# SSD output projection of a hybrid decoder layer: seven products of quarters in place of eight, with the sums of activations made by GpSimd group by group

## The chip, the cores and the metric

One core of a Trainium2 chip runs the whole program in one launch. The metric is the device time of one execution in microseconds (us). A core has a tensor engine (TensorE, PE in the rows; PEld is its weight loading), a vector engine (VectorE, DVE), a scalar engine (ScalarE, ACT), GpSimd (POOL) and SyncE (SP). Here SP only issues DMA transfers; POOL and ACT issue some too. Each engine works through its own instructions in order and waits on semaphores for the others.

## The reference

The reference is one decoder layer on x of 1024 tokens by 1024 channels: a Mamba-2 SSD branch and a latent-attention branch, merged by gates, then a gated MLP. The part that is edited:

```python
y_ssd = ssd_mixer(...) @ w_ssd_proj[i]       # (1024 tokens, 2048) @ (2048, 1024)
y_mla = mla_mixer(...) @ w_mla_proj[i]
g_ssd, g_mla = jnp.split(jax.nn.sigmoid(gates + gate_b[i]), 2, axis=-1)
x = x + (g_ssd * y_ssd + g_mla * y_mla) @ w_o[i]
```

`ssd_mixer` ends in an RMS norm over each of four groups of 512 channels: a group's 512 rows of the projection's input are final once its scan over the tokens is done.

## The kernel before

Activations lie with channels on the partitions and tokens along the row. A matrix product in f32 is made of three matmuls in f32r (`mm3`, L174): each operand is split into a rounded part `hi` and a rest `lo` (ACT casts, DVE or GpSimd subtracts, `split`, L152), and hi·hi, hi·lo and lo·hi are added in PSUM. The rows of TensorE therefore come in threes, L175 to L177, each 128x128 weights against 128x512 activations.

The stages around the change, in the order of time in the profile:

- **SSD scan** (to about 1262 us). Four groups of channels, each in eight chunks of 128 tokens (`ssd_steps`). TensorE is filled in between by "background" work: the convolution inputs of the next group, the z tiles, the attention's output projection (`mla_tiles`). The order within this stage is fixed by how many background steps `advance` takes per step of the scan; the instructions of each engine stand in the order in which the code emits them. When half a group's tokens are scanned, `ssd_finish(g, half)` sums squares, takes the inverse root (DVE, L119 to L125), transposes it (L955) and scales the group's four 128x512 tiles (L957). Half 0 of the last group is split at once and stays on chip; all other halves are stored to `y_d` in DRAM by SP (L965), four stores of 256 KB.
- **SSD output projection** (about 1253 to 1475). Eight output tiles of 128 channels for each half of the tokens. One tile is 16 steps over the 2048 input channels, 48 matmuls. Half 0 has its activations (`ya0`) loaded and split during the attention projection; its first tile runs as background while the last group is normalised (`first_ssd_tile`). Half 1's are loaded from `y_d` and split between the halves (`load_act`). Weights: `load_w` brings 256 KB pieces through two `wraw` buffers (L160) and splits them.
- **Gates and merge.** Each tile's result is multiplied by its gate (`gt`, loaded from `g_d` by GpSimd, L1214), the attention's part is added (`mt` from `m_d`, L1216) and the sum is split (`ma`, `m`).
- **w_o** for that half of the tokens: eight steps over channels for each half of the outputs, added to x (L1270), squares summed, the result `x2` stored to `x_d` (L1280). So the order is: projection half 0, w_o half 0, projection half 1, w_o half 1. The second norm's scaling of half 0 (`norm`, L255) is emitted ahead of w_o half 1, and reads and overwrites the tile that the store to `x_d` reads.
- **MLP up and down**, which already uses seven products of quarters (`Pair`, `w_sums`, `w_split`); its first raw weights are loaded by `w_raw` into the pool `up`.

The pool `up`, opened after the SSD stage, lies over memory that the stage's pool `dp` frees; what is loaded into it waits for whatever still uses that memory. Hardware DMA transfers of SP take turns on eight semaphore lanes: a transfer waits for the one eight before it, so at most eight are outstanding.

Of the kernel before, what the change touches and what calls it, by code (L numbers as in the profile page):

```python
# [9 lines left out]
F32 = mybir.dt.float32  # L10
# [62 lines left out]
def tile_hybrid_layer(ctx: ExitStack, tc: tile.TileContext, x, cols, cons, w_main, w_small, w_uq, w_ukv,  # L73
# [14 lines left out]
    l_d = dram.tile([4 * MH, 256], F32, name="l_d")  # L88
    y_d = dram.tile([2 * D, T], F32, name="y_d")
    z_d = dram.tile([2 * D, T], F32, name="z_d")  # L90
# [82 lines left out]
    def mm3(ps, a, b, first, last, **more):  # L173
        (ah, al), (bh, bl) = a, b  # L174
        PE.matmul(ps, lhsT=ah, rhs=bh, start=first, stop=False, **more)  # L175
        PE.matmul(ps, lhsT=ah, rhs=bl, start=False, stop=False, **more)  # L176
        PE.matmul(ps, lhsT=al, rhs=bh, start=False, stop=last, **more)  # L177

    def act_tile():
# [592 lines left out]
    with tc.tile_pool(name="dp", bufs=2) as dp, tc.tile_pool(name="psx", bufs=1, space=PSUM) as psx, \  # L772
# [166 lines left out]
        def ssd_finish(g, half):  # L939
# [16 lines left out]
            for j in range(4):  # L956
                V.scalar_tensor_tensor(x[:, j, s], x[:, j, s], col(CG_SSDG + 4 * g + j), np_,  # L957
                                       op0=ALU.mult, op1=ALU.mult)
# [35 lines left out]
        def mla_tiles():  # L994
# [11 lines left out]
            def y_step(j):  # L1006
# [5 lines left out]
                if j < 24 and j % 2 == 0:  # L1012
                    k = j // 2
                    raw = dp.tile([P, 512], F32, name="nb") if 4 <= k < 6 else \
                        dp.tile([P, 8, P], F32, name="abc", bufs=3).rearrange("p a b -> p (a b)")[:, 0:512] if k > 8 else \
                        lt.tile([P, 512], F32, name="lt")
                    staged.append(raw_load(y_d, k, hs_(0), raw))

# [32 lines left out]

        def first_ssd_tile():
            ws = [load_w(w_ssd[0, kp], [P, KD, P]) for kp in range(2)]
            ps = lin_tile()
            head.append(ps)
            for k in range(16):
                while ya0[k] is None:
                    yield False
                hi, lo = ws[k // KD]
                mm3(ps, (hi[:, k % KD, :], lo[:, k % KD, :]), (ya0[k][:, 0, :], ya0[k][:, 1, :]), k == 0, k == 15)  # L1060
                yield True

# [38 lines left out]
        w_eng[0] = V  # L1101
        background.append(first_ssd_tile())
        while fins:
# [65 lines left out]
    with tc.tile_pool(name="ep", bufs=2) as ep:  # L1169
        x2b = []  # L1170
        with tc.tile_pool(name="em", bufs=2) as em:
# [31 lines left out]

            m0 = [em.tile([P, 2, 512], F32R, name="ma", bufs=3) for _ in range(3)]
            for half in range(2):
                if half:
                    w_raw(q0, loaded)
                    w_raw(q1, loaded)
                s = hs_(half)
                ya = ya0 if half == 0 else [load_act(y_d, k * P, s) for k in range(16)]  # L1210
                ms = []
                for ct in range(8):
                    gt = em.tile([P, 512], F32, name="gt")
                    nc.gpsimd.dma_start(out=gt, in_=g_d[ct * P:(ct + 1) * P, s])  # L1214
                    mt = em.tile([P, 512], F32, name="mt")
                    nc.gpsimd.dma_start(out=mt, in_=m_d[ct * P:(ct + 1) * P, s])  # L1216
                    if half == 0 and ct == 0:
                        ps = head[0]
                    else:
                        ps = lin_tile()  # L1220
                        drain([steps([load_w(w_ssd[ct, kp], [P, KD, P]) for kp in range(2)], ya, ps, range(16), 16)])
                    if ct == 5:
                        loaded = last(mybir.EngineType.SP)
                    V.scalar_tensor_tensor(gt, gt, 1.0, ps, op0=ALU.add, op1=ALU.mult)
                    V.tensor_tensor(gt, gt, mt, op=ALU.add)  # L1225
                    m = em.tile([P, 2, 512], F32R, name="m", bufs=5) if ct >= 3 else \
                        em.tile([P, 2, 512], F32R, name="ma", bufs=3) if half else m0[ct]
                    S.mul(m[:, 0, :], gt, 0.5)
                    V.scalar_tensor_tensor(m[:, 1, :], gt, 0.5, m[:, 0, :].bitcast(F32), op0=ALU.mult, op1=ALU.subtract)
                    ms.append(m)  # L1230
                if half:
                    x0 = [x2b[0][:, i, :] for i in range(4)]
                    drain([norm(x0, x0, ep, x2ss[0])])
                big = ep.tile([P, 4, D], F32, name="x2")
                x2b.append(big)
                nc.sync.dma_start(out=big, in_=x[s, :].rearrange("(i p) c -> p i c", p=P))
                behind(loaded)
                sq4 = ep.tile([P, 4, 2], F32, name="sq4")
                x2ss.append(sq4)
                nq = 0  # L1240
                for ch in range(2):
                    banks = [bank6() for _ in range(4)]
                    qs = slice(ch * 512, (ch + 1) * 512)
                    for kp in range(4):
                        wh, wl = [wpool.tile([P, 2, 512], F32R, name=n) for n in ("whi", "wlo")]
# [6 lines left out]

                        if half and (ch, kp) in ((1, 0), (1, 1)):
                            q = pairs[kp]
                            q.a = w_split(q.r1, hp_tiles(), V)
                            w_sums(q, act_tile().rearrange("p a (b c) -> p (a b) c", c=P).bitcast(F32) if kp else None)
                        if half and (ch, kp) == (1, 3):
                            q2.a = hp_tiles()
# [4 lines left out]
                        for i in range(4):  # L1263
                            tk = slice(i * P, (i + 1) * P)
                            for k in range(2):
                                m = ms[2 * kp + k]
                                mm3(banks[i], (m[:, 0, tk], m[:, 1, tk]), (wh[:, k, :], wl[:, k, :]),
                                    kp == 0 and k == 0, kp == 3 and k == 1)
                            if kp == 3:
                                V.tensor_tensor(big[:, i, qs], banks[i], big[:, i, qs], op=ALU.add)  # L1270
                                junk = em.tile([P, 512], F32, name="junk", bufs=1)
# [4 lines left out]
                            if half and i % 2 and nq < KD:  # L1276
                                quarter("11" if nq < 4 else "21", nq % 4, h2_raw(nq, 0), act_tile(), G)
# [501 lines left out]
```

## Time and profile before

| | us |
|---|---|
| median of three runs | 2198.29 |
| lowest and highest | 2197.89, 2204.68 |
| profiled execution | 2203.12 |
| its span, first to last instruction | 2201.3 |
| TensorE busy | 2145.3 (97%) |
| DVE, ACT, GpSimd busy | 1446.8, 1064.3, 969.6 |

The mean granted clock of TensorE is 0.996 of full speed. A row of a timeline gives the start and duration in us, the engine, the line of the code, the operation with the names of its output and inputs, the shape, how often it is repeated back to back, and in brackets the engine's idle time before it with what ended it. A row of a group gives total busy us and the mean of one in ns, then the idle time before it by what ended it. A window's row gives each engine's busy us with its instruction count, then the granted clock, the mean busy share of the 16 DMA engines and their rate in GB/s. PE rows overlap (a matmul's row is longer than the distance to the next), so the distance between starts is what one costs. Of a DMA issue a row shows only the issuing instruction, except in the last part of the page, which gives the median from issue to landing.

### The profile page before, as it was taken

To read this page: it belongs to the slowest core of one execution; us is meant where nothing else is said; L and a number is where in the kernel's file an instruction comes from. 1 tells how busy PE (TensorE), PEld (TensorE's weight loads), DVE (VectorE), ACT (ScalarE), POOL (GpSimd) and SP (SyncE) were. 2 spreads that over 40 slices of the span, in tenths; PEclk is the share of its full clock that TensorE was granted. 3 is DMA by queue.
4 is the path that set the end of the run, shared out by engine and by line. 5 is a ranking of instruction groups with operands and counts; after the bars stand their busy time and mean duration, and the time that the engine had idled before them with its cause. 6 is when DMAs were issued, how large, how long until landed. Compare 5 with 4: busy or idle time off the path is not lost. (4 is left out here: it accounts for less than half of the span.)

```text
span 2201.3 us, 30448 instructions
## 1 busy us (share of the span) xinstructions
PE 2145.3 (97%) x10844; PEld 1713.8 (78%) x10844; DVE 1446.8 (66%) x2567; ACT 1064.3 (48%) x2034; POOL 969.6 (44%) x1049
## 2 busy tenths in 40 slices
PE   8999999999999999999999999999899999999999
PEld 7877776777777887778877787887678888877787
DVE  4466756575664469898877746545876676676762
ACT  5445454555454456656564424324655455554330
POOL 2344424432443237665456311013377777744430
PEclk9999999999999999999999999999999999999999
DMA  4221111111112224645266566542132333248642
GB/s 147 69 69 46 40 53 64 50 35 55 64 48 88 93 82 148 195 151 172 92 229 212 178 224 200 166 161 95 63 119 92 111 105 110 96 138 330 258 158 82
DMA packets 121767, 268.97 MB, mean 122 GB/s; under 512 B 13520, under 2 KB 25744, under 8 KB 121616
## 3 DMA queue, kind: packets, MB, share of 16 engines
q1 hardware_dynamic: 105600, 214.47, 29.0%
q0 software_dynamic: 14528, 49.29, 6.8%
q10 hardware_dynamic: 1488, 3.28, 0.4%
q8 instruction: 85, 1.39, 0.3%
q14 instruction: 66, 0.54, 0.1%
HBM read 201.45 MB, written 65.54 MB: 121 GB/s over the span
## 5 line engine op out<-in xcount | busy, mean ns | idle before, releaser
L175 PE MATMUL lin<-h,whi 128*128 128x512 f32 x1440 | 591.6, 411 | 1.5 <-DVE lt L330 1.5
L177 PE MATMUL lin<-h,wlo 128*128 128x512 f32 x1440 | 563.7, 391 | 0.0
L176 PE MATMUL lin<-h,whi 128*128 128x512 f32 x1440 | 562.4, 391 | 0.0
L175 PEld LDWEIGHTS lin<-h,whi 128*128 128x128 f32 x1440 | 270.6, 188 | 83.9 <-issue 33.8
L177 PEld LDWEIGHTS lin<-h,wlo 128*128 128x128 f32 x1440 | 270.4, 188 | 59.8 <-POOL wlo L154 0.4
L176 PEld LDWEIGHTS lin<-h,whi 128*128 128x128 f32 x1440 | 271.5, 189 | 53.2 <-issue 6.7
L154 POOL TENSOR_TENSOR wlo<-wraw,whi 128x512 fp32r<-128x512 f32 x134 | 193.0, 1458 | 169.3 <-ACT whi L153 165.7
L153 ACT CAST whi<-wraw 128x512 fp32r<-128x512 f32 x232 | 141.1, 619 | 260.0 <-PE lin L176 111.1
L664 POOL TENSOR_TENSOR acc<-acc,e 128x512 f32<-128x512 f32 (+3 forms) x80 | 78.8, 984 | 246.1 <-ACT e L659 223.7
L659 ACT ACTIVATE e<-s 128x512 f32<-128x512 f32 (+1 forms) x192 | 93.3, 492 | 153.7 <-DVE s L657 133.1
L1140 DVE TENSOR_TENSOR xlo<-ur,xhi 128x512 fp32r<-128x512 f32 (+1 forms) x41 | 83.0, 2024 | 60.9 <-ACT xhi L1139 60.9
L154 DVE TENSOR_TENSOR wlo<-wraw,whi 128x512 fp32r<-128x512 f32 x98 | 70.0, 725 | 75.1 <-ACT whi L153 74.7
L850 ACT ACTIVATE seg<-abc,acum 128x128 f32<-128x128 f32 x256 | 80.2, 390 | 47.1 <-PE yp L891 41.0
L175 PE MATMUL dps<-tq,h 128*128 128x512 f32 x242 | 96.8, 400 | 5.8 <-DVE xr L1601 3.5
L176 PE MATMUL dps<-tq,h 128*128 128x512 f32 x242 | 96.9, 400 | 0.8 <-DVE tq L154 0.8
L177 PE MATMUL dps<-tq,h 128*128 128x512 f32 x242 | 96.4, 398 | 0.0
L812 DVE SCALAR_TENSOR_TENSOR xg<-craw,cl,xg 128x1024 f32<-128x1024 f32 x48 | 73.7, 1536 | 27.4 <-ACT xg L810 26.9
L664 DVE TENSOR_TENSOR acc<-acc,e 128x512 f32<-128x512 f32 (+3 forms) x80 | 55.1, 689 | 37.1 <-ACT e L659 36.5
L1216 POOL DMA_DIRECT2D mt<-m_d x16 | 8.6, 539 | 147.1 <-DVE gt L1225 97.1
L154 DVE TENSOR_TENSOR h<-ar,h 128x1024 fp32r<-128x1024 f32 (+1 forms) x35 | 56.4, 1616 | 25.4 <-ACT h L153 25.3
L670 PE MATMUL pv<-e,vt 128*64 128x512 f32 (+3 forms) x384 | 72.9, 498 | 0.0
L629 DVE CUSTOM_DVE_ANT_0 s<-s,negw 128x128 f32<-128x128 f32 (+3 forms) x128 | 62.3, 495 | 13.5 <-PE s L627 13.4
(617 smaller groups left out, 5225.7 us busy)
## 6 DMA issues: line engine op xcount, KB each, us to landing
wraw<-in_w_main SPq DMA_DIRECT2D x112, 256.0 KB
ur<-in_w_up SPq DMA_DIRECT2D x44, 512.0 KB
ar<-f_d SPq DMA_DIRECT2D x34, 512.0 KB
abc<-ac_d POOLq DMA_DIRECT2D x32, 512.0 KB, 5.3
wraw<-in_w_ssd SPq DMA_DIRECT2D x64, 256.0 KB
f_d<-wraw POOLq DMA_DIRECT2D x33, 256.0 KB, 2.4
g_d<-lt SPq DMA_DIRECT2D x32, 256.0 KB
z_d<-lt SPq DMA_DIRECT2D x32, 256.0 KB
```

The costliest lines, as they stand in the source:

```text
L153: S.copy(hi, raw)
L154: (eng or V).tensor_sub(lo, raw, hi.bitcast(F32))
L175: PE.matmul(ps, lhsT=ah, rhs=bh, start=first, stop=False, **more)
L176: PE.matmul(ps, lhsT=ah, rhs=bl, start=False, stop=False, **more)
L177: PE.matmul(ps, lhsT=al, rhs=bh, start=False, stop=last, **more)
L629: V.tensor_tensor_reduce(ps[:, 0:w], ps[:, 0:w], negw[:, 512 - w:512], 1.0, 2 * NEG, ALU.add, ALU.max, nm[:, j, i:i + 1])
L659: S.activation(e[:, c0:512], ps[:, 0:w], AF.Exp)
L664: (V if hd else G).tensor_tensor(accs[hd][:, c0:512], accs[hd][:, c0:512], e[:, c0:512], op=ALU.add)
L670: PE.matmul(pv[hd * 64:(hd + 1) * 64, c0:512], lhsT=vt[:, j, hd * 64:(hd + 1) * 64], rhs=es[hd][:, c0:512], start=first, stop=last)
L812: V.scalar_tensor_tensor(c, raw[:, k:k + T], col(cw + k), c, op0=ALU.mult, op1=ALU.add)
L850: S.activation(seg[:, hd, :], abc[:, hd, :], AF.Relu, bias=acum[:, c, 8 * g + hd:8 * g + hd + 1], scale=-1.0)
L1140: eng.tensor_sub(lo, r, hi.bitcast(F32))
```

## The change

The product of w_ssd (1024 outputs by 2048 inputs) with the activations (2048 by 1024 tokens) is divided in two along each of the three sizes: output tiles 0 to 3 and 4 to 7, token halves, and two halves of the channels. The channels of every group are divided alike (tiles 0 and 1, tiles 2 and 3 of the group, `quarter_k`), so that each group contributes to both halves. Seven products of quarters with sums of them (a Winograd form of Strassen's method) replace eight. A product is 4 output tiles ("units") of 8 steps, 24 matmuls each.

- **Sums of activations.** In `ssd_finish(g, 1)`, GpSimd forms t3 = s12 − s22, t2 = s11 + t3, t4 = s21 − t2 and t1 = s22 − t2 in place in the group's tile, each 128x2x512, and issues a store of 512 KB for s22 and each sum to `t_d`. The four `y_d` stores of half 1 on SP go.
- **Sums of weights.** GpSimd makes them from raw quarters (`raw_q`), 128x1024 each: e2, e1, and in place the next two.
- **Order of products**: 1, 2, 6, 5, 3, 7, 4. Products 1, 2 and 4 take plain weights through `wraw` (`load_q`, rows of 1 KB); the others take a raw quarter or a sum, split as 128x1024. For product 2, `fetch` also loads three raw quarters for each of its four units, into `ur`, `ug`/`us` and `x2` buffers, three units ahead: 24 loads of 256 KB. The first two units of product 1 take the place of the first tile as background.
- **Results.** Products 1, 6 and 5 leave copies that the later ones add (`finish_unit`); gates are applied as quarters become complete.
- **w_o** halves then run back to back. Half 1 takes its steps in the order 2, 3, 0, 1; half 0's norm is emitted within it, in groups of four; the first transposes for the MLP start later, and the first raw MLP weights are loaded earlier.

```diff
@@ ssd_finish
-                else:
-                    nc.sync.dma_start(out=y_d[r0:r0 + P, s], in_=x[:, j, s])
+                elif half == 0:
+                    nc.sync.dma_start(out=y_d[r0:r0 + P, :], in_=x[:, j, s])
             if half:
+                s11, s21 = x[:, 0:2, 0:512], x[:, 2:4, 0:512]
+                s12, s22 = x[:, 0:2, 512:1024], x[:, 2:4, 512:1024]
+                def form(name, v, a=None, b=None, op=None):
+                    if op is not None:
+                        G.tensor_tensor(v, a, b, op=op)
+                    nc.gpsimd.dma_start(out=t_d[name][2 * g * P:2 * (g + 1) * P, :].rearrange("(j p) t -> p j t", p=P),
+                                        in_=v)
+                form("22", s22)
+                form("t3", s12, s22, s12, ALU.subtract)
+                form("t2", s11, s12, s11, ALU.add)
+                form("t4", s21, s21, s11, ALU.subtract)
+                form("t1", s22, s22, s11, ALU.subtract)
...
@@ the products
+            def raw_q(t, ct, h):
+                for kp in range(2):
+                    nc.sync.dma_start(out=t[:, 4 * kp:4 * kp + 4, :].rearrange("p (g j) c -> p g (j c)", j=2),
+                                      in_=quarter_w(ct, h, kp))
...
+            units = [(p, i) for p in (1, 2, 6, 5, 3, 7, 4) for i in range(4)]
+            source = {6: "t2", 5: "t1", 3: "22", 7: "t3", 4: "t4"}
...
+            def fetch(n):
...
+                if p == 2:
+                    raw_q(ur[i], i, 0)
+                    rs[p, i] = ring()
+                    raw_q(rs[p, i], i + 4, 0)
+                    raw_q(e1[:, i], i + 4, 1)
+                elif p == 3:
+                    rs[p, i] = ring()
+                    raw_q(rs[p, i], i, 1)
+            def prepare(n):
...
+                if p in (1, 2, 4):
+                    ws[p, i] = load_q(i + 4 if p == 4 else i, 0 if p == 1 else 1)
+                    if p == 2:
+                        G.tensor_tensor(e2[:, i], ur[i], rs[p, i], op=ALU.subtract)
+                    return
...
+            for n in range(2, 5):
+                fetch(n)
+            prepare(2)
+            for n in range(2, len(units)):
+                p, i = units[n]
+                fetch(n + 3)
+                prepare(n + 1)
...
+                for kk in range(KD):
+                    quarter_step(b, ws[p, i], forms[p][kk], kk, p in (1, 2, 7))
+                finish_unit(p, i)
...
@@ w_o
-                    drain([norm(x0, x0, ep, x2ss[0])])
+                    drain([norm(x0, x0, ep, x2ss[0], group=4)])
...
-                    for kp in range(4):
+                    for n_, kp in enumerate((2, 3, 0, 1) if half else range(4)):
```

SP, behind the scan, in the changed program (`wraw` are the plain weights of products 1 and 2; `ur`, `ug`, `us` and `x` the raw quarters, L1252; `lt` the sums read back). The two `wraw` rows after the last `x` row are the weights of the third unit of product 2:

```order
L191 DMA wraw<-in_w_ssd 128x2x256 x8
L205 DMA lt<-t_dt_78 128x512 x3
L1252 DMA ur_12833<-in_w_ssd 128x2x256 x2
L1252 DMA ug<-in_w_ssd 128x2x256 x2
L1252 DMA x_12831<-in_w_ssd 128x2x256 x2
...
L1252 DMA ug<-in_w_ssd 128x2x256 x2
L1252 DMA x_12831<-in_w_ssd 128x2x256 x2
L191 DMA wraw<-in_w_ssd 128x2x256 x2
L205 DMA lt<-t_dt_78 128x512 x2
```

The eight loads ahead are those of the last two units of product 1 and the first two of product 2; the 24 raw loads stand between them and the next pair. Before, SP had only `wraw` loads of the tiles in turn there.

GpSimd in the group after group 0, before (`st` is the scan's state, `abc` its next input, `wlo` the rest of a split weight, `zt` a z tile, `sq` and `sqs` sums of squares, `rb` the attention's scaling):

```order
L879 TENSOR_TENSOR st<-st,cdec 128x512
L788 DMA abc<-ac_d 128x1024
L154 TENSOR_TENSOR wlo<-wraw,whi 128x512
L796 DMA zt<-z_d 128x4x128
L154 TENSOR_TENSOR wlo<-wraw,whi 128x512
L915 TENSOR_TENSOR sq__9523<-sq__9523 128x256
L916 TENSOR_TENSOR sqs<-sq__9523 128x128
L980 TENSOR_TENSOR rb<-rb,nb 128x512
L879 TENSOR_TENSOR st<-st,cdec 128x512
L788 DMA abc<-ac_d 128x1024
```

and in the changed program, up to the state product:

```order
L900 TENSOR_TENSOR st<-st,cdec 128x512
L809 DMA abc<-ac_d 128x1024
L994 DMA t_d_76<-xg 128x2x512
L993 TENSOR_TENSOR xg<-xg 128x2x512
L155 TENSOR_TENSOR wlo<-wraw,whi 128x512
L994 DMA t_dt_79<-xg 128x2x512
L993 TENSOR_TENSOR xg<-xg 128x2x512
L936 TENSOR_TENSOR sq__9533<-sq__9533 128x256
L994 DMA t_dt_78<-xg 128x2x512
L993 TENSOR_TENSOR xg<-xg 128x2x512 x2
L994 DMA t_dt_80<-xg 128x2x512
L994 DMA t_dt_77<-xg 128x2x512
```

Four sums and five stores now stand between two state products; `sqs`, `rb`, `zt`, the second state product, the second `wlo` and the next `abc` follow them in this order.

Behind the last group, GpSimd's sums are followed by the gates' loads and the sums of weights:

```order
L994 DMA t_dt_80<-xg 128x2x512
L994 DMA t_dt_77<-xg 128x2x512
L1241 DMA gt<-g_d 128x512
L1243 DMA mt<-m_d 128x512
L1241 DMA gt<-g_d 128x512
L1243 DMA mt<-m_d 128x512
L1299 TENSOR_TENSOR x_12832<-ur_12833,ug 128x1024
```

The last store there, of t1, is one that SP's first raw load waits for.

More of the change, by code (lines that the diff above doesn't have):

```diff
@@ L1205, in tile_hybrid_layer @@
+            bigs = [ep.tile([P, 4, D], F32, name="x2") for _ in range(2)]
             for half in range(2):
+                nc.sync.dma_start(out=bigs[half], in_=x[hs_(half), :].rearrange("(i p) c -> p i c", p=P))
+            ms = ma + ml
+            for half in range(2):
+                s = hs_(half)
                 if half:
[L1207 to L1230, printed above, removed]
@@ L1235, in tile_hybrid_layer @@
+                big = bigs[half]
                 x2b.append(big)
[L1236 to L1237 removed]
                 sq4 = ep.tile([P, 4, 2], F32, name="sq4")
                 x2ss.append(sq4)
+                slot = 0
                 nq = 0
```

158 lines of the change are left out of this document (134 added, 24 removed).

## The prediction

> **What bounds the kernel now.** The page comes first: TensorE is busy for 97% of the span, so matmuls taken out come off the end, unless something they covered comes into the open.
>
> ```profile
> span 2201.3 us, 30448 instructions
> PE 2145.3 (97%) x10844; PEld 1713.8 (78%) x10844; DVE 1446.8 (66%) x2567; ACT 1064.3 (48%) x2034; POOL 969.6 (44%) x1049
> ```
>
> Then the timeline of TensorE around the edited stage. Two third-product matmuls lie 14 starts apart; the third row is the first matmul behind the transposes of the last group's norm.
>
> ```profile
> 1289.81 0.39 PE L177 MATMUL lin<-h,wlo 128*128 128x512 f32 x1
> ...
> 1292.99 0.39 PE L176 MATMUL lin<-h,whi 128*128 128x512 f32 x1
> ```
> ```profile
> 1260.68 0.48 PE L175 MATMUL lin<-h,whi 128*128 128x512 f32 x1
> ```
>
> One matmul costs (1292.99 − 1289.81) / 14 = 0.227 us, back to back; a unit of 24 costs 5.45 us. The windows say how much room there is beside it: columns are PE, PEld, DVE, ACT, POOL busy, the clock, the DMA engines' share and their rate.
>
> ```profile
> 928.00:948.00 20.00, 19.44 (x109) 14.97 (x108) 20.00 (x28) 12.17 (x25) 11.07 (x10) 1.00 0.53 174
> 1042.00:1062.00 20.00, 20.00 (x112) 15.78 (x111) 16.81 (x24) 13.60 (x27) 10.54 (x9) 1.00 0.50 165
> 1173.00:1193.00 20.00, 20.00 (x118) 15.87 (x116) 12.89 (x22) 9.38 (x18) 10.03 (x13) 1.00 0.75 243
> ```
> ```profile
> 1120.00:1130.00 10.00, 10.00 (x68) 8.19 (x67) 6.38 (x13) 7.49 (x18) 5.66 (x8) 1.00 0.94 303
> 1310.00:1320.00 10.00, 10.00 (x46) 8.29 (x45) 4.53 (x7) 2.75 (x5) 1.07 (x2) 1.00 1.01 392
> 1343.00:1366.00 23.00, 21.33 (x89) 15.80 (x88) 13.68 (x21) 12.02 (x20) 1.08 (x2) 1.00 0.74 240
> ```
>
> The first three are where groups 0, 1 and 2 are normalised (their half-1 stores leave at about 931, 1042 and 1173): DVE is full at the first, has 3.2 us of 20 free at the second, 7.1 at the third. The other three give DMA rates at full engines, and a stretch with 1.67 us of idle TensorE, in which half 1 of the activations is read back.
>
> **The change part by part.** *Matmuls.* 28 units of 24 make 672 in place of 768: 96 × 0.227 = **−21.8 us**. The read-back of half 1 goes, and its gap with it: **−1.7**.
>
> *The last group's sums and the weights behind them.* The raw weights of the second product (24 loads of 256 KB) go into buffers in the memory of the SSD stage's pool; the first of them therefore waits for every store of a sum, the last group's t1 too. All 24 stand on SP ahead of the two loads for the third unit of that product, unit 6 counted from 0. The rows that price this:
>
> ```profile
> L1140 POOL TENSOR_TENSOR wlo<-ur,whi 128x1024 fp32r<-128x1024 f32 x19 | 46.1, 2427 | 6.7 <-ACT whi L1139 6.7
> ...
> L1376 POOL DMA_DIRECT2D f_d<-wraw x33 | 18.2, 552 | 1.7 <-POOL ur L1150 0.9 <-POOL wraw L1374 0.6 <-POOL ug L1311 0.3
> ```
> ```profile
> L153 ACT CAST whi<-wraw 128x512 fp32r<-128x512 f32 x232 | 141.1, 619 | 260.0 <-PE lin L176 111.1
> ...
> L154 DVE TENSOR_TENSOR wlo<-wraw,whi 128x512 fp32r<-128x512 f32 x98 | 70.0, 725 | 75.1 <-ACT whi L153 74.7
> ...
> abc<-ac_d POOLq DMA_DIRECT2D x32, 512.0 KB, 5.3
> ...
> f_d<-wraw POOLq DMA_DIRECT2D x33, 256.0 KB, 2.4
> ```
> ```profile
> 1260.96 2.72 DVE L957 SCALAR_TENSOR_TENSOR xg<-xg,cl,np__12753 128x512 f32<-128x512 f32 x4 [0.81 <-PE np__12753 L955]
> ```
>
> The norm ends at 1260.96 + 2.72 = 1263.68. GpSimd then does four sums of 1024 columns and five issues: 4 × 2.43 + 5 × 0.55 = 12.5, to 1276.2. The last store lands 2.4 us (a 256 KB store) to 5.3 us (a 512 KB load) later; it is a 512 KB store, and I take about 3.8: 1280, bounds 1278.6 and 1281.5. From there 24 + 2 weight loads and about 5 gate loads move, 31 × 0.262 = 8.1 MB. At 392 GB/s that takes 20.7 us, at 303 it takes 26.8; the 392 window reads long rows and these rows are 1 KB pieces, so I take 345, 23.6 us. About 1.6 us of fixed delay (2.4 less 0.76 for 0.262 MB) and 0.62 + 0.73 for cast and subtraction bring unit 6's weights to 1280 + 23.6 + 1.6 + 1.3 = 1306.5. TensorE comes to it after units 1 to 5, at 1260.68 + 5 × 5.45 = 1287.9. **Stall +18.6**; bounds 1278.6 + 20.7 + 1.3 − 1287.9 = 12.7 and 1281.5 + 26.8 + 1.6 + 1.3 − 1287.9 = 23.3. Nothing in TensorE's order can fill it: unit 6 is next. Had the burst room, or stood behind those two loads, they would be covered like the loads of units 2 to 5, and this term would be zero.
>
> After such a wait the array restarts slowly. The chain of waits shows it behind a 6.75 us wait on a load: about 8 matmuls at 0.43, then 0.23.
>
> ```profile
> 1999.17 0.43 PE dps L177
> ...
> 2001.64 0.23 PE dps L177
> ```
>
> So 8 × 0.20 = **+1.6**. The Trainium skill's "TensorE: Matmul & The Clock Gate" (what's actually happening) puts half clock after about 3.4 us of idle and for about as long; that would be 8 × 0.21 here too, and it makes the cost the same for a stall of 13 or 23 us.
>
> *The sums of groups 0 to 2.* They enter GpSimd's queue in the middle of the scan. The timeline of the first, GpSimd first, then the three that wait for it:
>
> ```profile
> 932.35 1.29 POOL L154 TENSOR_TENSOR wlo<-wraw,whi 128x512 fp32r<-128x512 f32 x1 [3.42 <-ACT whi L153]
> 935.77 0.79 POOL L796 DMA_DIRECT2D zt<-z_d  x1 [2.13 <-DVE xg L905]
> 936.58 1.30 POOL L154 TENSOR_TENSOR wlo<-wraw,whi 128x512 fp32r<-128x512 f32 x1
> 937.82 0.75 POOL L915 TENSOR_TENSOR sq__9523<-sq__9523 128x256 f32<-128x256 f32 x1
> 938.64 1.33 POOL L916 TENSOR_TENSOR sqs<-sq__9523 128x128 f32<-128x128 f32 x1
> 939.94 2.27 POOL L980 TENSOR_TENSOR rb<-rb,nb 128x512 f32<-128x512 f32 x1
> 942.17 2.02 POOL L879 TENSOR_TENSOR st<-st,cdec 128x512 f32<-128x512 f32 x1
> 944.14 0.59 POOL L788 DMA_DIRECT2D abc<-ac_d  x1
> ```
> ```profile
> 944.01 1.26 DVE L864 TENSOR_TENSOR seg<-seg,sm__9576 128x1024 f32<-128x1024 f32 x1
> ...
> 947.97 0.67 DVE L881 TENSOR_TENSOR st<-st,sn 128x512 f32<-128x512 f32 x1
> ...
> 955.69 2.31 DVE L864 TENSOR_TENSOR seg<-seg,sm__9706 128x1024 f32<-128x1024 f32 x1
> ```
> ```profile
> 951.17 0.39 PE L177 MATMUL lin<-h,wlo 128*128 128x512 f32 x1
> ```
> ```profile
> 953.96 1.57 ACT L850 ACTIVATE seg<-abc,acum 128x128 f32<-128x128 f32 x5 [1.96 <-PE yp L891]
> ```
>
> The new order puts all nine sum and store instructions ahead of the state product (L879), of the second half of a weight split and of the load of abc. The norm of group 0 is done at about 933.5, between the first two rows. From there 12.5 us of sums and stores and 1.29 + 0.75 + 1.33 + 2.27 + 0.79 = 6.4 of what stood there end at 952.4; the product ends at 954.4, the split at 955.7, where abc is issued. DVE's state addition is then 954.4 − 947.97 = 6.4 late, TensorE's matmul at 951.17 is 4.5 late, and ACT's segment, which needs abc at 955.7 + 5.3 = 961.0, is 7.0 late. DVE has no room (20.00 of 20), so I take **+6**; with 1.3 us for rb and the product, as other 128x512 rows have it, the weights are 2.8 late, the lower bound. Behind group 1:
>
> ```profile
> 1043.90 0.59 POOL L788 DMA_DIRECT2D abc<-ac_d  x1
> ...
> 1057.05 2.04 POOL L879 TENSOR_TENSOR st<-st,cdec 128x512 f32<-128x512 f32 x1
> ```
> ```profile
> 1186.09 1.04 POOL L879 TENSOR_TENSOR st<-st,cdec 128x512 f32<-128x512 f32 x1
> ```
>
> From 1044.5, 12.5 and some 4.3 of like work put the product at 1061.3, 4.2 late; behind group 2 the same count gives 1190 for 1186.09. DVE's 3.2 and 7.1 us of room take most of it: **+1** and **+2**, together 9. Bounds for the three: +3, and the +18.8 worked out under the rivals.
>
> *Behind the products.* The first norm-scaled product of x2 half 0 stands in DVE's queue behind the wait for its 2 MB store:
>
> ```profile
> 1389.72 0.69 DVE L1270 TENSOR_TENSOR x<-dps,x 128x512 f32<-128x512 f32 x1
> ...
> 1397.94 1.42 DVE L255 TENSOR_SCALAR x<-x,nst 128x1024 f32<-128x1024 f32 x2 [4.37 <-DMA x_d<-x]
> ```
>
> Now, with the w_o halves back to back, half 1's third weight split is queued behind it. TensorE wants that split two steps of 24 matmuls after half 0's end, 10.9 us; from the last addition the scalings end 1397.94 + 4 × 0.71 − 1389.72 = 11.1 us later, and the split takes 0.73: **+1**, from +0.6 to +2.5. The other new work of the product stage (weight sums of 2.43 us, three a unit at most for the raw products; 40 activation splits) lies beside 5.45 us units; priced at nothing, and about 0.5 us a unit if DVE, fullest during the second product, falls behind.
>
> Sum: −21.8 − 1.7 + 18.6 + 1.6 + 9 + 1 = **+6.7**, on the profiled execution's 2203.1 (span 2201.3 and 1.8 around it). The median shown is 2198.3, 4.8 below; by it the forecast is **2205 us**, just at the mark from which a change can be told (0.3%, 6.6 us).
>
> **The rivals.** *A, the groups take the sums in for nothing.* GpSimd idles 3.42 and 2.13 us in the rows above; if the consumers' lateness runs out within the scan, 9 becomes 2 and the time 2198. Against it stands DVE at 20.00.
>
> *B, faster.* The burst, not the groups: at 392 GB/s from 1278.6 the stall is 12.7; with the groups at 2 and the rest as above, −23.5 + 12.7 + 1.6 + 2 + 0.6 = −6.6, 2191.7. It decides when unit 6's weights land before about 1300. For it: 24 loads in a row with eight outstanding keep the engines as full as in the 392 window. Against it: 303 in the other full window, and the gate loads.
>
> *C, the sums hold up DVE itself.* The same operation (L864) took 1.26 us at 944.01 and 2.31 at 955.69, when GpSimd ran
>
> ```profile
> 952.43 4.49 POOL L154 TENSOR_TENSOR wlo<-wraw,whi 128x512 fp32r<-128x512 f32 x2
> ```
>
> at 2.24 each in place of 1.29. If four sums of 2.43 hold DVE for all their 9.7 us, the first group costs 9.7, the second 9.7 − 3.2 = 6.5, the third 2.6: 18.8 in place of 9, +16.5, 2215. Against it: TensorE's work ahead covers part, and DVE reads PSUM in some of the operations there. The Trainium skill's "SBUF — State Buffer" (SBUF: two separate sides) has a lock for this: a DVE operation with two inputs in SBUF and a GpSimd operation that reads SBUF exclude each other for the whole instruction; the stretched pair agrees.
>
> **How the numbers follow.** Forecast 0.40, A 0.20, B 0.15, C 0.25. Range: B's 2191 less a little to C's 2215 and a little more: 2189 to 2217; the forecast's own range is 2200 to 2210. Slower: half of the forecast's 0.40 and C, 0.45. Faster: 0.12 of B and 0.03 of A, 0.15. Same: 0.40.
>
> **What would show it.** The first load of raw weights issued at about 1280 (wrong below 1275); one TensorE wait of 15 to 22 us before the third unit of the second product, ended by ACT, DVE or a wraw load, and half-clock matmuls behind it; pitch 0.227 elsewhere. In the groups, TensorE idle between 945 and 975 up by about 6, DVE's state addition late behind GpSimd, and less at 1055 and 1190. If idle before unit 6 is under 8 us, the time falls below 2192 and the burst reading is wrong; if idle in the groups exceeds 15, C holds.

## The result, and the profile after

| | us |
|---|---|
| before, median of 4 runs | 2198.09 |
| changed kernel, median of 4 runs (2232.51 to 2237.40) | 2234.58 |
| ratio, with its 95% interval | 1.016 (1.0138 to 1.0183) |
| its profiled execution, and its span | 2234.45, 2232.4 |

36.5 us slower by the medians, where about 6.7 slower was forecast, and outside the range of 2189 to 2217. The page shows that the matmuls did go, 96 of them, and that more than their time came back as waiting:

```profile
span 2232.4 us, 30306 instructions
...
PE 2130.3 (95%) x10748; PEld 1696.6 (76%) x10748; DVE 1529.4 (69%) x2543; ACT 1075.2 (48%) x2046; POOL 1062.7 (48%) x1101
```

DVE has 24 instructions fewer than before and is busy 82.6 us longer. That is the row to stop at.

Where the time is: the transposes of the eight norms are the same in both kernels and serve as marks (x4 is the four matmuls of one norm; the numbers behind the colon are shortest, median and longest in ns, then the first and last start in us). Before, then after; the rows are the last norm of group 0, the next one (half 0 of group 1), and the last of all:

```profile
L955 PE MATMUL np__9469<-cn,grr x4: 271/272/273, 924.8 to 925.1; 128*128 128x128 f32 x4
L955 PE MATMUL np__10090<-cn,grr x4: 271/272/273, 990.0 to 990.3; 128*128 128x128 f32 x4
...
L955 PE MATMUL np__12753<-cn,grr x4: 272/273/295, 1260.3 to 1260.7; 128*128 128x128 f32 x4
```
```profile
L976 PE MATMUL np__9474<-cn,grr x4: 271/272/273, 924.4 to 924.7; 128*128 128x128 f32 x4
L976 PE MATMUL np__10100<-cn,grr x4: 272/272/273, 1000.6 to 1000.9; 128*128 128x128 f32 x4
...
L976 PE MATMUL np__12773<-cn,grr x4: 273/273/293, 1276.7 to 1277.0; 128*128 128x128 f32 x4
```

Level until the first sums; 11.0 us lost behind group 0's (76.2 in place of 65.2), 16.4 by the last norm. The marks left out show 4.1 of it behind group 1 and 1.6 behind group 2. Behind the last mark TensorE's waits in the products are (line, what it waited for: us in all, times, longest):

```profile
PE dps L176 <- ACT whi L154: 23.0, 1, 23.0
PE dps L178 <- DVE wlo L155: 6.8, 4, 3.3
PE lin L178 <- DVE wlo L155: 3.7, 2, 1.9
```

(ACT casts the `hi` of an operand and DVE subtracts its `lo`, so these are waits on splits.) The 23.0 is the forecast's stall at unit 6. The other six, 10.5 us, were priced at nothing. The granted clock was half in parts of it; windows as before (PE, PEld, DVE, ACT, POOL, clock, DMA share, GB/s):

```profile
1310.00:1330.00 20.00, 0.17 (x1) 0.18 (x2) 14.86 (x10) 2.07 (x4) 17.61 (x11) 0.50 1.09 352
1330.00:1350.00 20.00, 15.34 (x47) 11.51 (x48) 19.97 (x9) 5.82 (x9) 19.12 (x8) 0.74 0.57 186
```

Some 28 matmuls, in three stretches from 1329.8, 1343.6 and 1360.3, started 0.43 us apart in place of 0.23: about 5.6 us. The sum for the profiled executions: −21.8 − 1.7 + 16.4 + 23.0 + 10.5 + 5.6 = 32.0, against 2232.4 − 2201.3 = 31.1 of span. In the second window nine DVE instructions take 19.97 us. This is the timeline of DVE there, and GpSimd's:

```profile
1329.81 5.34 DVE L155 TENSOR_TENSOR wlo<-wraw,whi 128x512 fp32r<-128x512 f32 x2 [3.61 <-ACT whi L154]
1335.07 5.68 DVE L155 TENSOR_TENSOR h<-lt,h 128x512 fp32r<-128x512 f32 x2
1340.67 5.60 DVE L155 TENSOR_TENSOR wlo<-wraw,whi 128x512 fp32r<-128x512 f32 x2
```
```profile
1329.44 2.37 POOL L1299 TENSOR_TENSOR x<-ur,us 128x1024 f32<-128x1024 f32 x1
1331.89 2.70 POOL L1303 TENSOR_TENSOR x<-x,x 128x1024 f32<-128x1024 f32 x1
1334.68 2.72 POOL L1305 TENSOR_TENSOR ur<-ur,x 128x1024 f32<-128x1024 f32 x1
```

A subtraction of 128x512 that took 0.73 us in the mean before takes 2.7 to 2.8, the length of a GpSimd sum: the two engines take turns. Behind group 0 it is worse. The same DVE operation before and after, then GpSimd and TensorE's one long wait after:

```profile
934.80 0.68 DVE L905 SCALAR_TENSOR_TENSOR xg<-zt,xg 128x512 f32<-128x512 f32 x1
```
```profile
934.39 6.78 DVE L926 SCALAR_TENSOR_TENSOR xg<-zt,xg 128x512 f32<-128x512 f32 x1
```
```profile
933.88 2.40 POOL L993 TENSOR_TENSOR xg<-xg 128x1024 f32<-128x1024 f32 x1
936.24 1.29 POOL L155 TENSOR_TENSOR wlo<-wraw,whi 128x512 fp32r<-128x512 f32 x1
937.47 0.73 POOL L994 DMA_DIRECT2D t_dt<-xg  x1
938.22 2.39 POOL L993 TENSOR_TENSOR xg<-xg 128x1024 f32<-128x1024 f32 x1
...
953.33 1.83 POOL L900 TENSOR_TENSOR st<-st,cdec 128x512 f32<-128x512 f32 x1
```
```profile
951.40 2.07 PE L895 MATMUL sn<-xde,bt 128*128 128x512 f32 x2 [8.22 <-DVE bt L884]
```

A DVE operation of 0.68 us stands for 6.78: over two sums, a weight split and a store issue of GpSimd, until GpSimd falls idle at 940.61. TensorE waits 8.22 us for a DVE copy queued behind this operation and seven more. GpSimd's state product, which the forecast had as the late one, runs at 953.3 to 955.2 (954.4 was counted), but nobody waits for it: DVE gets to the addition that uses it only at 959.16.

The windows from the first to the last of these marks, before and after, give the size:

```profile
924.80:1260.30 335.50, 327.57 (x2006) 262.52 (x2005) 276.85 (x458) 191.11 (x368) 177.02 (x173) 1.00 0.53 171
```
```profile
924.40:1276.70 352.30, 332.21 (x2007) 263.79 (x2005) 312.68 (x458) 190.49 (x367) 211.29 (x200) 0.99 0.53 177
```

The same 458 DVE instructions take 35.8 us more. The twelve sums in it are 12 × 2.4 = 29 us of GpSimd. TensorE's idle time, the length of the window less its busy time, goes from 7.9 to 20.1 us.

Two theories go into the experiments. H: a GpSimd sum and a DVE operation that reads two inputs from SBUF hold each other up. Q: what costs is the place in GpSimd's queue, as the forecast had it. Beside them B: unit 6 waits only because of the 24 loads ahead of its two.

Every experiment but the last three is one run. The kernel before ranged from 2196.5 to 2208.7 us over 14 runs of one chip, so a few us between single totals say little; the traces have to say it. The runs also reach their first norm, ahead of all sums, anywhere from 876.3 to 880.1 us, so the time between the marks (from group 0's last norm to the last of all: 335.5 us before, 352.3 in the changed kernel) measures the groups better than the last mark alone, and the time from the last mark to the end (941.0 and 955.7) measures the products with what follows them.

### The profile page after: what moved, and what is told of

It reads as the page before. It is cut to its first block, busy times and chain, and to the rows that moved or that the text cites. A ratio compares the mean times of both kernels' runs of the same rounds, so it can differ in the third digit from the quotient of the medians.

```text
span 2232.4 us, 30306 instructions
## 1 busy us (share of the span) xinstructions
PE 2130.3 (95%) x10748; PEld 1696.6 (76%) x10748; DVE 1529.4 (69%) x2543; ACT 1075.2 (48%) x2046; POOL 1062.7 (48%) x1101
## 3 DMA queue, kind: packets, MB, share of 16 engines
q1 hardware_dynamic: 112768, 214.47, 28.6%
q10 hardware_dynamic: 1488, 3.28, 0.4%
## 5 line engine op out<-in xcount | busy, mean ns | idle before, releaser
L176 PE MATMUL lin<-h,whi 128*128 128x512 f32 x1248 | 519.7, 416 | 1.4 <-ACT craw L829 0.9
L178 PE MATMUL lin<-h,wlo 128*128 128x512 f32 x1248 | 490.8, 393 | 4.3 <-DVE wlo L155 3.7
L177 PE MATMUL lin<-h,whi 128*128 128x512 f32 x1248 | 489.5, 392 | 0.0
L176 PEld LDWEIGHTS lin<-h,whi 128*128 128x128 f32 x1248 | 235.8, 189 | 78.7 <-issue 35.3
L178 PEld LDWEIGHTS lin<-h,wlo 128*128 128x128 f32 x1248 | 235.1, 188 | 58.1 <-DVE wlo L155 4.5
L177 PEld LDWEIGHTS lin<-h,whi 128*128 128x128 f32 x1248 | 236.4, 189 | 46.3 <-issue 7.3
L154 ACT CAST whi<-wraw 128x512 fp32r<-128x512 f32 x192 | 116.6, 618 | 187.0 <-PE lin L177 59.2
L176 PE MATMUL dps<-h,whi 128*128 128x512 f32 x244 | 97.0, 398 | 26.1 <-ACT whi L154 23.0
L176 PE MATMUL dps<-tq,h 128*128 128x512 f32 x242 | 97.1, 401 | 7.0 <-DVE xr L1750 3.4
L178 PE MATMUL dps<-h,wlo 128*128 128x512 f32 x244 | 97.3, 399 | 6.8 <-DVE wlo L155 6.8
L177 PE MATMUL dps<-h,whi 128*128 128x512 f32 x244 | 96.6, 396 | 0.0
L155 DVE TENSOR_TENSOR wlo<-wraw,whi 128x512 fp32r<-128x512 f32 x58 | 54.3, 957 | 36.4 <-ACT whi L154 36.3
L176 PEld LDWEIGHTS dps<-h,whi 128*128 128x128 f32 x244 | 46.8, 192 | 36.7 <-ACT whi L154 23.4
```

The source lines that it names most:

```text
L154: S.copy(hi, raw)
L155: (eng or V).tensor_sub(lo, raw, hi.bitcast(F32))
```

## Experiments on the sums of activations

**Sums on DVE, stores left on GpSimd.**

```diff
-                        G.tensor_tensor(v, a, b, op=op)
+                        V.tensor_tensor(v, a, b, op=op)
```

> The sums of activations are made by DVE in place of GpSimd, the stores stay on GpSimd. Theory H (a GpSimd sum and a DVE operation with two inputs in SBUF hold each other up, the sum for its whole 2.4 us): DVE does four sums of 1.25, 5 us, in place of being held for 9.7; the first group's lateness falls from 11 us to 5 or 6, the last norm's transposes start at 1268 to 1270 (1276.7 in the changed kernel, 1260.3 before), the plain weights' splits behind the last group take 0.7 us again in place of 1.9 to 2.1, and the total is 2216 to 2223. Theory Q (what is late is what stands behind the sums in GpSimd's queue): the stores still wait there for DVE, which is full and has 5 us more to do; the transposes stay at 1274 or later and only the tail gains, total 2228 or more.

Measured: 2226.0 us (before on the same chip 2203.3). Marks of this run, group 0's last norm, the next, and the last:

```profile
L976 PE MATMUL np__9474<-cn,grr x4: 271/272/273, 921.9 to 922.2; 128*128 128x128 f32 x4
L976 PE MATMUL np__10100<-cn,grr x4: 271/272/273, 990.9 to 991.2; 128*128 128x128 f32 x4
...
L976 PE MATMUL np__12773<-cn,grr x4: 273/273/294, 1269.7 to 1270.1; 128*128 128x128 f32 x4
```

Behind group 0: 69.0 us, 3.8 late in place of 11.0, though DVE has 5 us more to do. The last mark, 1269.7, is in H's range, but the total is between the two theories' numbers, and the run reached group 0's norm 2.9 us sooner than the kernel before: between the marks it takes 347.8 us, 12.3 more than before, where the changed kernel takes 16.8 more. In that window DVE is busy 296.1 us, 16.6 less than in the changed kernel, with twelve operations more; that is H. But 7.5 of the 12.3 us that stay are one wait behind group 2's sums, and that is Q's kind:

```profile
PE lin L176 <- ACT sq__11887 L935: 7.5, 1, 7.5
```

```profile
1182.56 1.23 DVE L993 TENSOR_TENSOR xg<-xg 128x1024 f32<-128x1024 f32 x1 [5.91 <-DMA t_d<-xg]
```

ACT's square waits 9.05 us for DVE's L926 at 1183.70. That stands behind DVE's fourth sum, which overwrites s22 and so waits for the store of s22; GpSimd issues that store at 1175.83, 5 us after the norm, behind other work. The square does not wait for GpSimd itself, as the next expectation has it.

**The stores on SP as well.**

```diff
-                    nc.gpsimd.dma_start(out=t_d[name]...
+                    nc.sync.dma_start(out=t_d[name]...
```

> As the run with DVE's sums of activations, and the stores of the sums go to SP in place of GpSimd. Theory: what was left of the groups' lateness there (9.4 us by the last norm's transposes, 7.5 of it one TensorE wait in the last group behind a square that waited for GpSimd) was GpSimd's queue standing behind the stores, which wait for DVE. Then that wait goes, the transposes start at 1262 to 1265 and the total is 2216 to 2220. If DVE's own 5 us a group is what cost it: the transposes stay at 1268 or later, total 2224 or more.

Measured: 2224.0 (before 2202.2). The 7.5 us wait is gone. TensorE's stall at unit 6 is 14.2 in place of 20.6; in this run one of unit 6's two loads was issued at 1299.31, ahead of the last six raw loads. But the last mark is at 1269.8, and the time between the marks, 347.4 us, is no shorter: the waits on DVE's copies are 7.9 us (6.7 in the first experiment), and 3.9 on a DVE addition is new. That is the branch in which DVE's own 5 us a group is what is left, not GpSimd's queue. This part varies: four kernels with this same code in the groups (this one, and three further down) take 339.8 to 347.4 us between the marks. The four kernels that leave these sums on GpSimd in one piece (the changed one, and three further down) take 350.4 to 352.8, so the two ranges do not meet.

**Sums spread over the scan.** In groups 0 to 2 a `yield` ahead of each sum.

> In groups 0 to 2 the four sums are emitted one scan step apart, so that no more than one or two sums stand ahead of a state product, a weight split or an abc load in GpSimd's queue; the work is the same. Theory Q: the first group's lateness falls from 11 us to 3 or less and the last norm's transposes start at 1266 or before; total about 2224. Theory H: the same GpSimd time still holds up a DVE that has no room; the transposes stay between 1273 and 1279, total within 4 us of 2234.

Measured: 2253.8, worse than either theory said, so it decides nothing between them. The interval behind group 0 fell to 71.0 us (5.8 late), but by the code the finish of the next half waits in the same list behind the sums, so its norm moved back too: the intervals behind it are 70.8 for 48.7 and 113.9 for 72.8. The edit moved more than it should.

**Fills in place of sums.** GpSimd writes zeros twice for each sum, and reads nothing; the sums are left out.

```diff
-                        G.tensor_tensor(v, a, b, op=op)
+                        for _ in range(2):
+                            G.memset(v, 0.0)
```

> In place of each of the 16 sums of activations GpSimd fills the same 128x2x512 twice with zeros (so the output is not the reference's): its queue, its stores and their order stay, it writes but reads nothing of SBUF. Theory H (it is the sum's reading that holds DVE): DVE's operations between 930 and 960 keep their 0.7 to 1.3 us, the 8.2 us wait of TensorE there goes, and the first group is at most 4 us late though GpSimd's instructions stand ahead of the state product as before. Theory Q (the place in GpSimd's queue costs): if the fills take about as long as the sums, the first group stays 9 to 11 us late.

Measured: 2225.6. Behind group 0 the interval is 996.5 − 929.0 = 67.5 us, 2.3 late, and the 8.2 us wait is gone. DVE and GpSimd there:

```profile
939.03 0.68 DVE L926 SCALAR_TENSOR_TENSOR xg<-zt,xg 128x512 f32<-128x512 f32 x1
...
943.96 1.27 DVE L833 SCALAR_TENSOR_TENSOR chan<-craw,cl,chan 128x1024 f32<-128x1024 f32 x1
...
945.95 6.18 DVE L885 TENSOR_TENSOR seg<-seg,sm__9590 128x1024 f32<-128x1024 f32 x1
```
```profile
943.97 0.95 POOL L994 MEMSET xg<- 128x1024 f32 x1
...
946.24 1.31 POOL L1016 TENSOR_TENSOR rb<-rb,nb 128x512 f32<-128x512 f32 x1
947.50 2.54 POOL L155 TENSOR_TENSOR wlo<-wraw,whi 128x512 fp32r<-128x512 f32 x2
949.99 1.04 POOL L900 TENSOR_TENSOR st<-st,cdec 128x512 f32<-128x512 f32 x1
```

The DVE operation that stood for 6.78 takes 0.68 again, and one that runs beside a fill from end to end (943.96) keeps its 1.27; beside four reading GpSimd operations in a row one DVE operation stands for 6.18. The DVE busy time between the marks is 286.3 for the same 458 instructions, 26.3 less than in the changed kernel. That is H. It is not a clean test of the total, nor of Q: a fill is 0.95 to 0.98 us, so two are shorter than a sum, and a fill needs no sum ahead of it, so that GpSimd's order came out another way. Only four of group 0's eight fills stand behind its norm. The run lost time in other intervals (52.1 us ahead of group 0's last norm, where it was 45.6, and 56.9 for 48.7 behind the next); its last mark is at 1273.6.

## Experiments on the products

**Sums of weights left out.** The products take the raw quarters as they are.

```diff
-                    if p == 2:
-                        G.tensor_tensor(e2[:, i], ur[i], rs[p, i], op=ALU.subtract)
...
-                if p == 6:
-                    G.tensor_tensor(v, v, e2[:, i], op=ALU.subtract)
...
+                if p == 7:
+                    v = ur[i]
```

> The 16 sums of weights are left out (the products take the raw quarters, so the output is not the reference's); loads, splits and order stay. Theory H: DVE's 128x512 operations between 1310 and 1350, 2.7 to 2.8 us each there, take 0.7 again; TensorE's waits on wlo behind the stall (8.3 us in four) go to under 1; the stall of 23 us stays within 2 us; total 2224 to 2228. If DVE is slow there because of the load traffic: the durations and waits stay, total within 3 us of 2234.

Measured: 2223.2 (before 2203.3). The stall stays, the waits on wlo fall from 10.5 to 2.7, and DVE's rows at the same place read:

```profile
PE dps L176 <- ACT whi L154: 22.6, 2, 22.5
PE dps L178 <- DVE wlo L155: 2.7, 3, 2.0
```
```profile
1328.90 1.36 DVE L155 TENSOR_TENSOR wlo<-wraw,whi 128x512 fp32r<-128x512 f32 x2 [14.39 <-ACT whi L154]
1330.22 1.30 DVE L155 TENSOR_TENSOR h<-lt,h 128x512 fp32r<-128x512 f32 x2
```

0.65 to 0.68 us each in place of 2.7 to 2.8, with the same loads running. H, and not the traffic; of the 2.7 us of waits one of 2.0 stands ahead of the stall, beside the last group's sums, which stay here. From the last mark to the end it is 946.3 us in place of 955.7.

**The plain weights of units 6 and 7 ahead of 12 raw loads each** (an order between the issues on SP; the sum e2 is emitted behind them).

```diff
-            for n in range(2, 5):
-                fetch(n)
             prepare(2)
...
-                fetch(n + 3)
                 prepare(n + 1)
+                if n + 1 in (6, 7):
+                    w = last(mybir.EngineType.SP)
+                    for j in (2 * n - 6, 2 * n - 5):
+                        fetch(j, w)
+                        G.tensor_tensor(e2[:, j - 4], ur[j - 4], rs[2, j - 4], op=ALU.subtract)
```

> The plain weights of units 6 and 7 are issued ahead of 12 raw loads each. Theory B (unit 6 waits only because 24 loads stand ahead of its two): the wait of 23 us falls to under 4 us, and the total to 2212 to 2216. Theory H beside B: the wait falls just as far, but the sums of weights now run while DVE splits for units 7 to 12, so that waits on wlo and on split activations grow from 8 us to 15 or more; total 2220 to 2228.

Measured: 2232.4, beside 2232.5 to 2237.4 for the changed kernel, and from the last mark to the end 956.9 us beside 955.7: no gain. B was right that the 24 loads make most of the stall, and wrong on what that is worth:

```profile
PE dps L178 <- DVE wlo L155: 9.8, 4, 4.0
PE lin L177 <- DVE h L155: 7.0, 1, 7.0
PE dps L176 <- ACT whi L154: 7.0, 2, 3.8
PE lin L176 <- ACT h L154: 3.5, 1, 3.5
```

23.0 became 7.0 in two waits (under 4 was expected), and 9.8 + 7.0 + 3.5 of waits on splits stand where 10.5 stood: the sums, which ran during the stall, now run while DVE has to split. This is H's branch, with a total above its 2220 to 2228.

**The same with the sums of weights on DVE** (`V.tensor_tensor` in the four places).

> The plain weights of units 6 and 7 ahead of 12 raw loads each, as before, and the 16 sums of weights on DVE in place of GpSimd. Theory H: a sum holds DVE for 1.25 us in place of 2.5 or more, so TensorE's waits in the products (some 30 us in that run, without the sums on GpSimd) fall by 10 to 15: total 2218 to 2224. If DVE is simply full there, the waits stay about as long: total 2229 to 2235.

Measured: 2212.3 (before 2202.2), 20 us below the run before it (10 to 15 was expected); from the last mark to the end 932.9 us in place of 956.9. In the products:

```profile
PE dps L176 <- ACT whi L154: 6.8, 2, 3.9
...
PE dps L178 <- DVE wlo L155: 2.4, 2, 2.0
PE lin L177 <- DVE h L155: 0.8, 1, 0.8
```

Waits on splits from 20.3 to 3.2. Sixteen sums more on DVE make DVE's results come earlier: a sum costs it 1.22 us when it does it, and 2.5 or more when GpSimd does.

**Everything on DVE and SP, and six raw loads behind the weights of each of units 4 to 7**; then the same with the sums of weights on GpSimd.

```diff
+                if n + 1 in (4, 5, 6, 7):
+                    fetch(n + 1, last(mybir.EngineType.SP))
+                    V.tensor_tensor(e2[:, n - 3], ur[n - 3], rs[2, n - 3], op=ALU.subtract)
```

> Sums of activations on DVE with SP's stores, sums of weights on DVE, and six raw loads behind the plain weights of each of units 4 to 7. If both causes (the burst, and GpSimd's sums holding DVE) are the whole loss, the groups cost 4 to 5 us, unit 6 waits under 4 us, and the total is 2195 to 2202, no slower than the kernel before. If DVE's total work in products 2 and 6 is too long for their 44 us (some 10 us a unit of product 2 against 5.45), 10 to 15 us of waits on DVE stay: 2205 to 2212.

> As the run with six raw loads behind each unit's weights, but the sums of weights stay on GpSimd. Theory H: they hold DVE for some 2.5 us each while it splits and finishes; 8 to 15 us more of waits on DVE's splits than with the sums on DVE: total 8 to 15 above that run. If GpSimd's sums cost nothing beside DVE: within 3 us of it or below it.

Measured: 2203.9 and 2214.4 (before 2202.2). The pair differs only in who makes the weight sums: 10.5 us, as H said, although the one with GpSimd came 3.9 us earlier to the products; from the last mark to the end it is 934.5 and 948.9, 14.4 us. With both causes taken out, the kernel is back at the time before, and no lower: the groups still cost 8.9 us (344.4 between the marks), and four waits on plain weights in product 2, 7.2 us, remain while the DMA engines are nearly full or full (share 0.85 from 1280, 1.02 to 1.08 from 1290 to 1320).

**Raw loads earlier, and later.** The same kernel with the raw loads one unit earlier; then the sums and stores of group 2 back on GpSimd; then, with that, the raw loads at units 5 to 8 (six behind the weights of units 5 and 6 each, and twelve behind those of unit 7; the expectation counts them one unit further on):

```diff
+                if n + 1 in (5, 6, 7, 8):
+                    fetch(n, last(mybir.EngineType.SP))
```

> As the run with six raw loads behind each of four units' weights, everything on DVE and SP, but the raw loads one unit earlier, right behind the stores of the sums. There the first raw load was issued 8 us after the last store, and TensorE lost some 9 us in waits on weights of product 2 and 4 at half clock while the DMA engines were full. If it is the burst's late start: these waits fall to under 4 us and the time to 2193 to 2198, faster than the kernel before. If the bytes are too many for product 2 wherever they start: within 3 us of that run's 2204.

> As the last, but the sums and stores of group 2 alone stay on GpSimd, where DVE had 7 us of 20 free before. Theory H: no difference beyond 3 us from the last; if DVE's added 5 us is what made the third group 4 us late in two runs, 2 to 4 us faster.

> As the last, but the raw loads two units later, six behind the weights of each of units 6 and 7 and twelve behind those, so that the plain weights of units 4 to 6 have the queue to themselves and the raw quarters arrive during products 2 and 6. If unit weights of product 2 waited because of what stands ahead of them on SP: TensorE's waits on these weights fall from 10 us to under 4 and the time to 2197 to 2201, level with or below the kernel before. If the bytes are too many wherever they stand: the waits move to products 6's weights and the time stays within 3 us of 2205.

Measured as medians of 5, 10 and 6 runs, beside 14, 14 and 9 of the kernel before: earlier 2210.1, ratio 1.004 (1.0025 to 1.0054); with group 2 on GpSimd 2204.9, 1.0018 (1.0007 to 1.003), its last mark at 1262.6 in place of 1266.6 (for group 2, then, GpSimd was no worse a place for the sums; the intervals of the two ratios overlap); later **2193.7** beside 2202.0, **0.9965 (0.9949 to 0.9981)**. Earlier raw loads were no gain: TensorE's waits on plain weights were 10.3 us. The last is faster than both kernels, by 0.35% against the one before. Its waits in the products:

```profile
PE dps L176 <- ACT whi L154: 7.5, 4, 2.8
...
PE dps L178 <- DVE wlo L155: 0.4, 1, 0.4
```

These fell less than was expected (to under 4), and the time fell more (2197 to 2201 was expected). Its last mark is at 1264.4 and its span ends at 2195.9, so the products and what follows take 931.5 us, where they took 941.0 before. Of the 23.5 us that the matmuls and the gap are worth, some 9.5 arrive, and the groups take 5.7 of them (341.2 us between the marks).

## Why the prediction was wrong

- **96 matmuls, −21.8, and the gap, −1.7.** Right in count (10844 to 10748) and in price (of the two rows that give it, the second is of L176 and not of the third product; 14 starts is right). The last experiment shows that part of it can be had.
- **Stall at unit 6.** Right in place and in its main cause: 23.0 us for 18.6, inside the bounds 12.7 to 23.3. (The lower bound leaves out the 1.6 us of fixed delay that the upper one has; with it 12.7 is 14.3, and rival B's 2191.7 is 2193.3.) The start was wrong. From the end of the norm, 1280.1, to the first raw load, 1301.3, are 21.2 us, where 16.3 were counted. TensorE came to unit 6 26.8 us after the norm (24.2 counted), and unit 6 began 28.6 us after the first raw load (26.5 counted; the rate was 352 GB/s from 1310 to 1330, where 345 was taken): 18.6 + 4.9 + 2.1 − 2.6 = 23.0. The SP rows show what set the start: not the store of t1, but the eight plain-weight loads ahead of the burst, which fill 26 us. SP's row ahead of the first raw load ends at 1300.91, so that at most 0.35 us is left for waits on the stores. The longest of SP's waits are on DVE's subtractions (the row covers 1250 to 1340; 14.1 us of it, in five waits, lie among these eight loads), which run beside the last group's sums.

```profile
1273.42 25.89 SPq L191 DMA_DIRECT2D wraw<-in_w_ssd  x8
...
1301.26 2.24 SPq L1252 DMA_DIRECT2D ur<-in_w_ssd  x2
```
```profile
SPq L191 <- DVE wlo L155: 21.8, 10, 4.0
```

  With the last group's sums on DVE, in the first experiment, the first raw load is issued at 1285.67, 12.6 us after the norm's end at 1273.1.
- **Half clock, +1.6.** Right for one restart (some ten matmuls at 0.43, about 2 us); it came three times, 5.6 us: behind the 23.0 us, and behind waits on wlo of 3.28 and 1.93, the last clearly shorter than the 3.4 us of idle that the prediction names for it.
- **The sums of groups 0 to 2, +9.** This step failed. The size was 16.4 (11.0, 4.1 and 1.6 behind the three groups, where 6, 1 and 2 were taken), and the mechanism named, consumers of GpSimd's queue that come late, was not the one: the state product was as late as counted and nobody waited for it; TensorE waited 0.6 us in all for GpSimd's weight splits between the marks, and ACT's segment, at 962.79, waited for TensorE and not for abc. What was late was DVE, held by the sums.
- **"The other new work ... priced at nothing, and about 0.5 us a unit."** This failed too: 10.5 us of waits on splits, from the weight sums on GpSimd. The reckoning looked at DVE's own durations and not at what GpSimd does to them. It is the largest single miss: of the 25.3 us between 6.7 and the sum of 32.0 it is 10.5, the groups 7.4, the stall 4.4 and half clock 4.0, less the 1 us of the norm, which is not in that sum.
- **Norm of half 0, +1.** At most 0.9 us of waits on wlo in w_o; no run took this term by itself.
- **The rivals.** C had the mechanism (the row of 2.31 us for 1.26), and 18.8 for the groups against 16.4; it stopped at the groups. The sign set for it, more than 15 us of idle TensorE in the groups, is met by the 20.1 us between the marks, though not by the 12.2 that came on top of the 7.9 before. With the sizes measured since, 4.9 for the late start of the raw loads and 10.5 for the splits, its 2215 becomes 2230. B put the gain in a shorter stall; the run with the plain weights ahead of the raw loads shows that taking most of the stall away brings nothing by itself (2232.4). A did not happen.

One sentence of the description ahead has to be put right: the instructions of an engine do not stand in the order in which the code emits them. The code emits six raw loads ahead of the plain weights of each of units 2 to 5; on SP all 24 stand behind those eight plain loads. What orders them so stays open.

## What to carry to other kernels

Before work is given to an idle GpSimd, look at what DVE does at that moment: in these traces a GpSimd operation that reads SBUF can hold a DVE operation with two inputs in SBUF for its whole length and longer, so most of the 128x1024 sums were cheaper on a DVE that was already full (1.22 us) than on a GpSimd that was not (2.4 and more, taken from both). Where DVE had room, in group 2, it made no clear difference. A kernel in which the critical engine is TensorE can still be bound by who splits its operands. And when a burst of loads is moved, count what its stall was covering: work that ran for nothing inside the wait will run beside something else afterwards.

## What the runs showed that was not expected

DVE does not always get its turn between two GpSimd operations: one operation of 0.68 us stood for 6.78 over two sums, a weight split and a store issue, another of 1.22 for 6.18 over four shorter ones, and each ended within its own length (0.56 and 1.10 us) of the end of the last of GpSimd's operations there. At other places the two took turns, 2.7 to 2.8 us a piece. The Trainium skill's "SBUF — State Buffer" (SBUF: two separate sides) says that whichever of the two starts first has the ports for the whole instruction; the runs agree, and show that the one that waits can be passed over more than once. The section's limit to operations with two inputs in SBUF agrees too. In the changed kernel this DVE operation, whose first input is in PSUM, kept its 0.68 us beside GpSimd's sums:

```profile
947.19 0.68 DVE L876 TENSOR_TENSOR xdt<-xp,dtt 128x512 f32<-128x512 f32 x1
```
```profile
943.60 5.87 POOL L993 TENSOR_TENSOR xg<-xg 128x1024 f32<-128x1024 f32 x2
```

And fills, which read nothing, did not hold DVE (1.27 us for an operation beside one of 0.95).
